# A two-layer diffusion backbone on one core: the squares of the output projections recorded as tasks, and three places moved at the end

## The chip, the cores and the metric

The kernel runs on one core of one Trainium2 chip, as one program. The metric is the device time of one execution in microseconds (us), the median over several executions. Five engines work in parallel, each through its own instructions in order: TensorE (PE, with its weight loads PEld), VectorE (DVE), ScalarE (ACT), GpSimd (POOL), and SyncE (SP), which issues nearly all DMA transfers. An instruction that waits holds up everything behind it on its engine.

## The reference

128 context tokens and 512 latent tokens of width 2048 go through two layers and a last norm. In each layer:

```python
h = rms_norm(x, norm_g[l]) * (1.0 + scale) + shift
y, side = even_mixer(...)  # layer 0: window attention || gated linear attention, times silu(gate)
y, side = odd_mixer(...)   # layer 1: neighbourhood attention || spatial-gating MLP, times silu(gate)
x = x + gate * (y @ w_out[l])
...
y_prompt = rms_norm(x, final_norm_g)

def rms_norm(x, g, eps=1e-6):
    xf = x.astype(jnp.float32)
    y = xf * lax.rsqrt(jnp.mean(xf * xf, axis=-1, keepdims=True) + eps)
    return (y * g.astype(jnp.float32)).astype(x.dtype)
```

The change touches the line `x = x + gate * (y @ w_out[l])`, called the output projection here, the sum of the squares of its result, which the next norm needs, and the last norm. Everything is in float32. The outputs are the two normed results and the keys, values and states of the context.

## The kernel before

**Layout.** Features lie on the 128 partitions, tokens on the free axis: an activation is KT = 16 tiles of 128 x 640 (128 context and 512 latent tokens). A float32 product is made from three passes of a faster format: every operand is split into a high part (`acth`, `whi`, made by ACT) and a low part (`actl`, `wlo`, made by POOL or DVE as the difference), and PE computes hi*hi, hi*lo and lo*hi.

**Weights.** SP loads weights into `wraw` or `rs`; ACT writes `whi`, POOL or DVE writes `wlo`. Both lie in a ring of 2560 columns, so a split can run ahead of PE only as far as PE has freed room. For most pairs of output chunks the kernel uses a Strassen-like scheme (`spair`) with sums of weights, which DVE makes (`wraw<-rs`, `rs<-wraw,rs`, 128 x 768), and sums of activations (`eh`, `el`).

**Folding and reloading.** For this scheme six tiles of the second half of the activations are overwritten ("folded"); their old values (`acth` and `actl`) are kept in DRAM (`bh_dram`, `bl_dram`). `unfold` reloads the six pairs when a stage ends, and sets a flag `uf0` to `uf5` for each; the matmuls that need them come behind the flag.

**Order.** The program is recorded by hand into fixed orders, engine by engine. A planner (`Pace`) keeps an estimated clock for each engine; `tick` is called between matmuls, and lets generator tasks (`spawn`) record their next steps. A task may wait for a flag (`wait`), for data by the planner's clock (`until`), or for an engine to be not too far ahead (`calm`). `need(flag)` lets tasks run, in the recording, until the flag is set. All of this sets only the order of instructions; on the chip they wait for semaphores.

**Output projection.** `out_proj` records 16 output tiles f, as n = 0 to 15. `out_evac` makes two functions for each: `pre` loads the tile of x, and `evac` takes the finished halves from PSUM (`pa`: first 320 tokens, `pb`: the rest), lets DVE write y = gate * p + x into `Y[n % 8]`, stores y, and has `square` record ACT's square and POOL's addition to `ssq` at once. In the profile a square is `arena<-Y` on ACT (128x320), the addition `arena<-arena` on POOL.

**The end.** The last pair of outputs of layer 1 runs through `hpair`, which splits the tokens into a part of 384 and one of 256 and finishes the first part before the second. After each part the task `final(half)` is spawned: it sums the squares over partitions with a matmul against `ones`, computes rstd with Ln and Exp on ACT (their function table is loaded by `tables` if another is active), scales the 16 tiles on DVE and POOL, and writes `o_y`. `reload` fetches tiles that had gone to DRAM. `final(1)` begins behind the flag `prescaled`, which `final(0)` sets at its tile 13 of 0 to 15.

Of the kernel before, what the change touches and what calls it, by code (L numbers as in the profile page):

```python
# [13 lines left out]
AF = mybir.ActivationFunctionType  # L14
ALU = mybir.AluOpType
# [4 lines left out]
KT = D // 128  # L20
# [15 lines left out]
NY = 8  # L36
# [203 lines left out]
class Trunk:  # L240
# [889 lines left out]
    def unfold(self):  # L1130

        nc = self.nc
        for i, j in enumerate(JT):
            for x, y in zip((self.ah, self.al), self.keep):
                self.dma(x[:, j, CW:].bitcast(U32), y[:, j, :].bitcast(U32))
                yield
            self.flags.add(f"uf{i}")
        self.flags.add("unfold")
        self.folded = False
        yield  # L1140
# [828 lines left out]
    def out_evac(self, l, n, f, xsrc, spill):  # L1969
        nc = self.nc  # L1970
        box = {}

        def square(y, c):
            if l == 1 and f == KT - 1:
                nc.scalar.activation(self.sq[:, : c.stop - c.start], y[:, c], AF.Square)
            else:
                self.ssq_add(self.ssq, y, f, self.sq if self.cut == CUT else self.sqs.next(), c)

        def squares(y):
            if n == KT - 1:  # L1980
                yield from self.wait("squares")
            for q, s in ((slice(0, HT), self.sqs.next()), (slice(HT, T), self.sqs.next())):
                yield from self.wait("x1:14")
                yield from self.calm(2.0, "a")
                nc.scalar.activation(s, y[:, q], AF.Square)
                yield from self.until(s)
                yield from self.calm(4.0, "v")
                nc.vector.tensor_tensor(self.ssq[:, q], self.ssq[:, q], s, ALU.add)
                yield
            self.flags.add("squares")  # L1990

        def evac(pa, pb):
            G, at = self.G[l], self.cut
            y = self.Y[:, n % NY, :]
            if pa is not None:
                if n < NY:
                    self.clear(f"Y{n}", "C", "R")
                x = box["x"]
                nc.vector.scalar_tensor_tensor(
                    y[:, 0:NCTX], pa[:, 0:NCTX], G[:, f, 0:1], x[:, 0:NCTX], ALU.mult, ALU.add  # L2000
                )
                nc.vector.scalar_tensor_tensor(
                    y[:, NCTX:at], pa[:, NCTX:at], G[:, f, 1:2], x[:, NCTX:at], ALU.mult, ALU.add
                )
                if pb is None:
                    square(y, slice(0, at))
            if pb is not None:
                x = box["x"]
                nc.vector.scalar_tensor_tensor(
                    y[:, at:T], pb[:, 0 : T - at], G[:, f, 1:2], x[:, at:T], ALU.mult, ALU.add  # L2010
                )
                if l == 0 or n < NY:
                    self.dma(spill[:, f, :], y)
                if l == 0 and n >= KT - 2:
                    return squares(y)
                if pa is not None:
                    square(y, slice(0, at))
                square(y, slice(at, T))

        def pre():  # L2020
            x = box["x"] = self.xr.next()
            self.dma(x, xsrc[:, f, :])

        return pre, evac
# [144 lines left out]
    def program(self):  # L2169
        nc, tc, d, Y = self.nc, self.tc, self.d, self.Y  # L2170
# [25 lines left out]
        def do(f):  # L2196
            acts.append(("f", f))
# [144 lines left out]
        for kv in range(2):  # L2342
# [26 lines left out]
            for h in range(4 * kv, 4 * kv + 4):  # L2369
                if kv and h != 5:  # L2370
                    i = max(h - 5, 0)
# [37 lines left out]
        def out_proj(l, xsrc, sp):  # L2409
            for i, f in enumerate(range(KT) if l else OUT0):  # L2410
                pre, ev = self.out_evac(l, i, f, xsrc, sp)
                add(wout[l, f], 128, False, pre, ev)
                if i == 1:
                    pair("k", STEPS, f"y{l}", f"uo{l}")
                elif i == KT - 3:
                    pairs((KT - 4) // 2)
# [139 lines left out]
        for i in range(2):  # L2556
            y = lambda i=i: L[f"gy{i}"]
# [3 lines left out]
        for n, i in enumerate(GATES):  # L2561
            y = Y[:, n % NY, :]
# [20 lines left out]
        acts.append(k)  # L2583
        do(lambda: self.need("ada_g1"))
        out_proj(1, spill, ysp)
        do(lambda: self.spawn(self.reload()))
        r = acts.pop()
        pair("h", self.final)
        h = acts.pop()
# [56 lines left out]
    def final(self, half):  # L2646
        nc, d, L = self.nc, self.d, self.L
        c = slice(CUT, T) if half else slice(0, CUT)
        n = c.stop - c.start
        t, u = (m[:, :n] for m in L["ms"])  # L2650
        if half:
            yield from self.wait("prescaled")
        p = self.sm()[:, :n]
        r = self.rstd[:, c]
        yield from self.until(self.ssq[:, c])
        self.mm(p, self.ones, self.ssq[:, c], stop=False)
        yield from self.until(self.sq[:, :n])
        self.mm(p, self.ones, self.sq[:, :n], start=False)
        if not half:
            yield 0.8  # L2660
        self.rms(r, p, t)
        q = self.sm()[:, :n]
        nc.vector.scalar_tensor_tensor(q, t, 1.5, r, ALU.add, ALU.mult)
        if half:
            nc.scalar.activation(u, t, AF.Copy, bias=1.5)
            nc.gpsimd.tensor_tensor(u, u, r, ALU.mult)
            self.flush()
        else:
            nc.scalar.activation(u, q, AF.Copy)
            self.flags.add("fr")  # L2670
            yield from self.wait("reload")
        at = 0
        for k in range(KT):
            y, g = self.x2(k)[:, 0, c], self.fg[:, k : k + 1]
            if k in self.POOLED:
                if not half:
                    yield from self.calm(1.5, "a")
                    nc.scalar.activation(self.x2(k), self.x2(k), AF.Copy, scale=g)
                nc.gpsimd.tensor_tensor(y, y, u, ALU.mult)
            else:  # L2680
                nc.vector.scalar_tensor_tensor(y, y, g, q, ALU.mult, ALU.mult)
            if half and (k % 2 or k == 0):
                eng = (nc.sync, self.tc.nc.scalar)[(k + 1) // 2 % 2]
                eng.dma_start(d["o_y"][:, at : k + 1, c], self.x2(at, k + 1 - at)[:, :, c])
                at = k + 1
            elif k % 2 and not half:
                self.dma(d["o_y"][:, k - 1 : k + 1, c], self.x2(k - 1, 2)[:, :, c])
            if not half:
                if k == self.POOLED[-1]:
                    self.flags.add("prescaled")  # L2690
                yield 0.3
        self.flags.add(f"final{half}")
        yield
# [164 lines left out]
```

## Time and profile before

| | |
|---|---|
| median of 3 executions | 2102.5 us (2102.18 to 2102.93) |
| the profiled execution | 2104.64 us, of it span 2102.8 us |
| TensorE clock granted | 0.996 on average |
| busy: PE, DVE, ACT, POOL | 2052.0, 1305.9, 1078.3, 1301.4 us |
| DMA | 340.18 MB, mean 162 GB/s |
| chain that ended last, by engine | PE 79%, DMA 7%, DVE 6%, POOL 3%, issue 3%, ACT 2% |

In a row of the timeline stand the start and the duration in us, the engine, the line, the operation, out<-in with shapes, the count of merged instructions, and in brackets the idle time of the engine before it and who ended it. L214 and L397 are lines of helpers that record every operation, so rows are told apart by their tiles. The first output projection runs from about 880 to 1060 us, the second from about 1890 us to the end.

### The profile page before, as it was taken

To read this page: it belongs to the slowest core of one execution; us is meant where nothing else is said; L and a number is where in the kernel's file an instruction comes from. 1 tells how busy PE (TensorE), PEld (TensorE's weight loads), DVE (VectorE), ACT (ScalarE), POOL (GpSimd) and SP (SyncE) were. 2 spreads that over 40 slices of the span, in tenths; PEclk is the share of its full clock that TensorE was granted. 3 is DMA by queue.
4 is the path that set the end of the run, shared out by engine and by line. 5 is a ranking of instruction groups with operands and counts; after the bars stand their busy time and mean duration, and the time that the engine had idled before them with its cause. 6 is when DMAs were issued, how large, how long until landed. Compare 5 with 4: busy or idle time off the path is not lost.

```text
span 2102.8 us, 40256 instructions
## 1 busy us (share of the span) xinstructions
PE 2052.0 (98%) x14345; PEld 2000.7 (95%) x14345; DVE 1305.9 (62%) x3034; ACT 1078.3 (51%) x2485; POOL 1301.4 (62%) x1090
## 2 busy tenths in 40 slices
PE   7999999999999999999999999999999999999997
PEld 6899999999999999999999999999999999999996
DVE  4746586676465664787376878787454444466434
ACT  5645565554566866543564434444444544454443
POOL 4656565355455563888755656555655577767884
PEclk9999999999999999999999999999999999999998
DMA  9966343335465544565634454444222344363426
GB/s 362 389 218 207 120 140 123 116 116 175 149 200 173 171 162 149 175 211 181 227 126 129 131 167 152 137 149 148 97 75 94 105 134 131 120 224 116 139 93 240
DMA packets 192841, 340.18 MB, mean 162 GB/s; under 512 B 20896, under 2 KB 70144, under 8 KB 192640
## 3 DMA queue, kind: packets, MB, share of 16 engines
q1 hardware_dynamic: 191296, 336.45, 48.4%
q8 instruction: 112, 1.84, 0.4%
q10 hardware_dynamic: 1344, 1.17, 0.2%
q14 instruction: 89, 0.73, 0.1%
HBM read 303.03 MB, written 31.88 MB: 159 GB/s over the span
## 4 chain that ended last, share of the span: by engine, by line
PE 79%; DMA 7%; DVE 6%; POOL 3%; issue 3%; ACT 2%; SPq 1%; ACTq 0%; POOLq 0%; DVEq 0%
PE bank L397 76%; POOL wlo L214 2%; PE bank L402 2%; DVE arena L214 1%; DVE adas L214 1%; DVE Y L214 1%; DMA adas<-gateT 1%; DMA more<-ada 1%; DVE bank L214 1%; ACT arena L214 1%; DMA Y<-xT 1%; DMA adas<-ada 1%; SPq L431 1%; PE bank L1426 1%; POOL actl L214 0%
## 5 line engine op out<-in xcount | busy, mean ns | idle before, releaser
L397 PE MATMUL bank<-acth,whi 128*128 128x320 f32 (+3 forms) x3320 | 1020.9, 318 | 7.3 <-ACT bc L214 3.0
L397 PE MATMUL bank<-acth,wlo 128*128 128x320 f32 (+3 forms) x3320 | 993.9, 310 | 3.2 <-POOL wlo L214 3.0
L397 PE MATMUL bank<-actl,whi 128*128 128x320 f32 (+3 forms) x3320 | 993.2, 310 | 1.1 <-DMA actl<-bl_dram 1.1
L214 POOL TENSOR_TENSOR wlo<-wraw,whi 128x512 fp32r<-128x512 f32 (+1 forms) x446 | 564.5, 1278 | 388.9 <-ACT whi L214 302.3
L397 PEld LDWEIGHTS bank<-acth,whi 128*128 128x128 f32 (+1 forms) x3320 | 617.1, 189 | 16.2 <-ACT bc L214 4.4
L397 PEld LDWEIGHTS bank<-acth,wlo 128*128 128x128 f32 (+1 forms) x3320 | 617.2, 189 | 4.7 <-POOL wlo L214 4.7
L397 PEld LDWEIGHTS bank<-actl,whi 128*128 128x128 f32 (+1 forms) x3320 | 617.2, 189 | 3.2 <-DMA actl<-bl_dram 1.6
L214 POOL TENSOR_TENSOR wlo<-rs,whi 128x384 fp32r<-128x384 f32 x370 | 409.2, 1125 | 190.8 <-ACT whi L214 154.3
L214 ACT ACTIVATE whi<-wraw 128x512 fp32r<-128x512 f32 (+1 forms) x456 | 260.7, 587 | 93.0 <-PE bank L397 66.4
L214 ACT ACTIVATE whi<-rs 128x384 fp32r<-128x384 f32 x370 | 183.3, 517 | 59.4 <-PE bank L397 51.2
L397 PE MATMUL bank<-eh,wlo 128*128 128x322 f32 (+1 forms) x666 | 206.8, 311 | 2.2 <-POOL wlo L214 2.2
L397 PE MATMUL bank<-eh,whi 128*128 128x322 f32 (+1 forms) x666 | 209.0, 314 | 0.0
L397 PE MATMUL bank<-el,whi 128*128 128x322 f32 (+1 forms) x666 | 206.8, 310 | 0.0
L214 DVE TENSOR_TENSOR wraw<-rs 128x768 f32<-128x768 f32 x74 | 99.1, 1339 | 131.6 <-DMA rs<-w_odd 46.6
L214 POOL TENSOR_TENSOR prod<-adas,mixrow 128x512 f32<-128x512 f32 x94 | 123.6, 1324 | 84.4 <-ACT prod L214 59.1
L214 DVE CUSTOM_DVE_ANT_0 adas<-adas,bank,partg 128x256 bf16<-128x256 f32 (+1 forms) x290 | 156.2, 539 | 12.0 <-DMA adas<-ada_g 4.6
L214 ACT ACTIVATE arena<-arena,bc 128x512 f32<-128x512 f32 (+4 forms) x189 | 97.8, 538 | 76.4 <-DVE arena L214 71.3
L397 PEld LDWEIGHTS bank<-eh,wlo 128*128 128x128 f32 x666 | 125.5, 188 | 3.5 <-POOL wlo L214 3.5
L397 PEld LDWEIGHTS bank<-el,whi 128*128 128x128 f32 x666 | 125.8, 189 | 0.0
L397 PEld LDWEIGHTS bank<-eh,whi 128*128 128x128 f32 x666 | 125.5, 188 | 0.1
L214 DVE TENSOR_TENSOR bank<-bank,sums 128x320 f32<-128x320 f32 (+1 forms) x148 | 70.7, 493 | 72.8 <-PE bank L397 56.3
L214 DVE CUSTOM_DVE_ANT_0 adas<-adas,bank,part 128x512 bf16<-128x512 f32 x142 | 105.6, 744 | 9.5 <-DMA adas<-ada 6.9
(221 smaller groups left out, 2467.7 us busy)
## 6 DMA issues: line engine op xcount, KB each, us to landing
wraw<-w_even SPq DMA_DIRECT2D x176, 256.0 KB, 3.4
adas<-ada_g SPq DMA_DIRECT2D x128, 256.0 KB, 3.6
adas<-ada SPq DMA_DIRECT2D x128, 256.0 KB, 3.6
rs<-w_odd SPq DMA_DIRECT2D x50, 384.0 KB, 3.2
wraw<-w_odd SPq DMA_DIRECT2D x74, 256.0 KB, 3.6
wraw<-w_out SPq DMA_DIRECT2D x60, 256.0 KB, 3.5
rs<-w_odd SPq DMA_DIRECT2D x50, 256.0 KB, 3.9
Y<-ada SPq DMA_DIRECT2D x24, 512.0 KB, 7.7
```

The source lines that it names most:

```text
L214: return f(*args, **kw)
L397: self.nc.tensor.matmul(out, lhsT, rhs, start=start, stop=stop, **kw)
L402: self.nc.tensor.transpose(out, in_, self.ident[:k, :k])
L431: self.nc.sync.dma_start(out, in_)
L1426: nc.tensor.matmul(o, c, w, start=j < 4, stop=j >= 12)
```

## The change

There are four edits. (1) For the first 12 of 16 outputs, each half's square becomes a task (`late`) of its own: it waits for the square before it, for y, and for ACT and then POOL to be not far ahead by the planner's clock. `evac` records, ahead of overwriting a slot of Y, that its squares are done, and ahead of the last four outputs that all tasks are. (2) `unfold` yields after a pair, not after each of its two transfers. (3) The Ln/Exp table is loaded where `reload` is spawned. (4) `final(1)` begins behind `final0`, the end of `final(0)`, instead of `prescaled`.

```diff
@@ unfold
             for x, y in zip((self.ah, self.al), self.keep):
                 self.dma(x[:, j, CW:].bitcast(U32), y[:, j, :].bitcast(U32))
-                yield
             self.flags.add(f"uf{i}")
+            yield
@@ out_evac
         def square(y, c):
-            if l == 1 and f == KT - 1:
+            if n < KT - 4:
+                self.spawn(late(y, c, 2 * n + (c.start > 0)))
+            elif l == 1 and f == KT - 1:
                 nc.scalar.activation(self.sq[:, : c.stop - c.start], y[:, c], AF.Square)
             else:
                 self.ssq_add(self.ssq, y, f, self.sq if self.cut == CUT else self.sqs.next(), c)
+
+        def late(y, c, i):
+            yield from self.wait("ssq" if i == 0 else f"sq{l}:{i - 1}")
+            yield from self.until(y[:, c])
+            yield from self.calm(1.0, "a")
+            if i < 2:
+                nc.scalar.activation(self.ssq[:, c], y[:, c], AF.Square)
+            else:
+                s = self.sqs.next()
+                nc.scalar.activation(s, y[:, c], AF.Square)
+                yield from self.until(s)
+                yield from self.calm(1.5, "g")
+                nc.gpsimd.tensor_tensor(self.ssq[:, c], self.ssq[:, c], s, ALU.add)
+            self.flags.add(f"sq{l}:{i}")
+            yield
@@ out_evac, evac
+            if n >= KT - 4:
+                self.need(f"sq{l}:{2 * KT - 9}")
             y = self.Y[:, n % NY, :]
             if pa is not None:
                 if n < NY:
                     self.clear(f"Y{n}", "C", "R")
+                    self.flags.add("ssq")
+                else:
+                    self.need(f"sq{l}:{min(2 * (n - NY) + 1, 2 * KT - 9)}")
@@ program
         out_proj(1, spill, ysp)
-        do(lambda: self.spawn(self.reload()))
+        do(lambda: [self.tables(), self.spawn(self.reload())])
@@ final
         if half:
-            yield from self.wait("prescaled")
+            yield from self.wait("final0")
```

Three places of the new order. PE's order is the same in both. First, ACT at the start of the second output projection (`arena_8164<-Y` are squares, `whi` weight splits, `acth<-bank` high parts of folded activations, `sums` a copy of a product). Before:

```order
L214 ACTIVATE arena_8164<-Y 128x320 x2
L214 ACTIVATE acth<-bank_69 128x320
L214 ACTIVATE whi<-rs_8159 128x384
L214 ACTIVATE sums_8160<-bank_67 128x320
L214 ACTIVATE whi<-wraw 128x384 x2
L214 ACTIVATE whi<-rs_8159 128x384 x2
L214 ACTIVATE arena_8164<-Y 128x320
L214 ACTIVATE whi<-rs_8159 128x384 x2
```

And in the change:

```order
L214 ACTIVATE acth<-bank_69 128x320
L214 ACTIVATE whi<-rs_8159 128x384
L214 ACTIVATE sums_8160<-bank_67 128x320
L214 ACTIVATE whi<-wraw 128x384 x2
L214 ACTIVATE whi<-rs_8159 128x384
L214 ACTIVATE acth<-bank_69 128x320
L214 ACTIVATE whi<-rs_8159 128x384 x3
L214 ACTIVATE whi<-wraw 128x512
L214 ACTIVATE whi<-wraw 128x384
L214 ACTIVATE arena_8164<-Y 128x320
```

The squares of the first outputs have left the splits of the first Strassen pair; the first one now stands behind them.

Second, SP at the last reload of pairs (`acth<-bh_dram` and `actl<-bl_dram` are one pair, `wraw<-w_out` a load of weights, `arena<-x1T_dram` one of x). From the third pair on, before:

```order
L431 DMA actl<-bl_dram 128x320
L431 DMA wraw<-w_out 128x512
L431 DMA acth<-bh_dram 128x320
L431 DMA arena_8164<-x1T_dram 128x640
L431 DMA actl<-bl_dram 128x320
L431 DMA wraw<-w_out 128x512
L431 DMA acth<-bh_dram 128x320
L431 DMA wraw<-w_out 128x512
L431 DMA actl<-bl_dram 128x320
L431 DMA acth<-bh_dram 128x320
L431 DMA wraw<-w_out 128x512
L431 DMA actl<-bl_dram 128x320
```

And in the change:

```order
L431 DMA actl<-bl_dram 128x320
L431 DMA arena_8164<-x1T_dram 128x640
L431 DMA acth<-bh_dram 128x320
L431 DMA actl<-bl_dram 128x320
L431 DMA acth<-bh_dram 128x320
L431 DMA actl<-bl_dram 128x320
L431 DMA acth<-bh_dram 128x320
L431 DMA actl<-bl_dram 128x320
L431 DMA arena_8164<-x1T_dram 128x640
L431 DMA wraw<-w_out 128x512 x3
```

The pairs stand together, and the weight loads come behind them.

Third, the end, on ACT (a piece of the difference: the table load, the splits of the last weights, the squares of the first part, 128x384, its rstd and its scaling):

```order
+L526 ACT_TABLE_LOAD
 L214 ACTIVATE whi<-wraw 128x512 x6
 L214 ACTIVATE arena_8164<-Y 128x384 x2
 L214 ACTIVATE whi<-wraw 128x512
-L526 ACT_TABLE_LOAD
 L214 ACTIVATE rstd<-bank_74,eps 128x384
 L214 ACTIVATE rstd<-rstd 128x384
 L214 ACTIVATE arena_8164<-bank_72 128x384
+L214 ACTIVATE whi<-wraw 128x512
 L214 ACTIVATE rs_8159<-rs_8159,small 128x640
```

The table load has moved ahead of seven splits, and one split ahead of the first scaling. On DVE (`Y<-Y,small,bank_72` are rows of the first part, those of 256 the second part), before:

```order
L214 SCALAR_TENSOR_TENSOR Y<-bank_68,G_99,arena_8164 128x256
L214 SCALAR_TENSOR_TENSOR Y<-Y,small,bank_72 128x384 x2
L214 SCALAR_TENSOR_TENSOR arena_8164<-rstd 128x256
L214 SCALAR_TENSOR_TENSOR arena_8164<-bank_73,arena_8164 128x256
L214 SCALAR_TENSOR_TENSOR bank_74<-arena_8164,rstd 128x256
L214 SCALAR_TENSOR_TENSOR rs_8159<-rs_8159,small,bank_74 128x256 x3
L214 SCALAR_TENSOR_TENSOR arena_8164<-arena_8164,small,bank_74 128x256 x2
L214 SCALAR_TENSOR_TENSOR adas<-adas,small,bank_74 128x256
L214 SCALAR_TENSOR_TENSOR Y<-Y,small,bank_74 128x256 x5
L214 SCALAR_TENSOR_TENSOR Y<-Y,small,bank_72 128x384
```

And in the change:

```order
L214 SCALAR_TENSOR_TENSOR Y<-bank_68,G_99,arena_8164 128x256
L214 SCALAR_TENSOR_TENSOR Y<-Y,small,bank_72 128x384 x3
L214 SCALAR_TENSOR_TENSOR arena_8164<-rstd 128x256
L214 SCALAR_TENSOR_TENSOR arena_8164<-bank_73,arena_8164 128x256
L214 SCALAR_TENSOR_TENSOR bank_74<-arena_8164,rstd 128x256
```

The last row of the first part has moved ahead of the second norm, and its write with it.

## The prediction

> **What bounds the kernel now.** I read the page first, for the shares, then the busy time by stretches of 50 us, then the timeline of TensorE (PE) for every matmul that waited, then the timelines of ScalarE (ACT), GpSimd (POOL), VectorE (DVE) and the sync queue (SP) around those matmuls.
>
> ```profile
> span 2102.8 us, 40256 instructions
> PE 2052.0 (98%) x14345; PEld 2000.7 (95%) x14345; DVE 1305.9 (62%) x3034; ACT 1078.3 (51%) x2485; POOL 1301.4 (62%) x1090
> ```
>
> PE is busy for 98% of the span, so only its gaps, and what comes before its first and after its last matmul, can be won. By stretches (columns: length, PE, PEld, DVE, ACT, POOL busy, clock, DMA share, GB/s):
>
> ```profile
> 950.00:1000.00 50.00, 48.36 (x328) 47.84 (x327) 37.78 (x81) 18.59 (x42) 42.03 (x39) 1.00 0.54 177
> 1900.00:1950.00 50.00, 48.85 (x329) 48.09 (x328) 26.98 (x44) 22.28 (x51) 42.94 (x39) 1.00 0.40 133
> 1950.00:2000.00 50.00, 50.00 (x343) 50.00 (x342) 20.14 (x30) 20.90 (x46) 43.84 (x40) 1.00 0.38 129
> ```
>
> The first two rows lie in the two output projections, which the change touches, and PE has gaps there at full clock; in the third row, the same work later on, it has none, with POOL as busy. So the gaps are matters of order, not of throughput. Every matmul behind a wait, from the first output projection to the last multiplication of weights (in brackets: idle time, and what ended it):
>
> ```profile
> 889.47 0.41 PE L397 MATMUL bank<-eh,wlo 128*128 128x320 f32 x1 [1.02 <-POOL wlo L214]
> 911.58 0.41 PE L397 MATMUL bank<-eh,wlo 128*128 128x320 f32 x1 [0.28 <-POOL wlo L214]
> 917.93 0.41 PE L397 MATMUL bank<-acth,wlo 128*128 128x320 f32 x1 [0.78 <-POOL wlo L214]
> 965.40 0.42 PE L397 MATMUL bank<-eh,wlo 128*128 128x320 f32 x1 [0.86 <-POOL wlo L214]
> 971.76 0.41 PE L397 MATMUL bank<-acth,wlo 128*128 128x320 f32 x1 [0.78 <-POOL wlo L214]
> 1916.74 0.43 PE L397 MATMUL bank<-acth,wlo 128*128 128x320 f32 x1 [1.06 <-POOL wlo L214]
> 2068.09 0.44 PE L397 MATMUL bank<-actl,whi 128*128 128x384 f32 x1 [0.42 <-DMA actl<-bl_dram]
> 2069.61 0.45 PE L397 MATMUL bank<-actl,whi 128*128 128x384 f32 x1 [0.64 <-DMA actl<-bl_dram]
> 2084.93 0.38 PE L397 MATMUL bank<-acth,wlo 128*128 128x256 f32 x1 [0.41 <-POOL wlo L214]
> ```
>
> Six wait for a weight's low part (wlo) in the projections, two for a reloaded low part of an activation (actl), one for a wlo in the last part. A wait costs more than its idle time, since the matmul behind it starts slowly. The matmuls before and after the 2068.09 one:
>
> ```profile
> 2067.16 0.33 PE L397 MATMUL bank<-acth,wlo 128*128 128x384 f32 x1
> 2067.34 0.33 PE L397 MATMUL bank<-acth,whi 128*128 128x384 f32 x1
> 2068.36 0.33 PE L397 MATMUL bank<-acth,wlo 128*128 128x384 f32 x1
> ```
>
> Starts are 0.18 us apart without a wait. Here the two steps around the wait take 0.75 and 0.27, together 0.66 over the usual 0.36, for an idle time of 0.42: each wait costs its idle time and 0.24.
>
> **Edit 1: the squares as tasks.** Now ACT squares a half of an output at once, and POOL adds it to ssq. ACT and POOL serve their instructions in order, and the weight splits stand behind the square. Around the waits at 917.93 and 1916.74:
>
> ```profile
> 915.50 0.47 ACT L214 ACTIVATE arena<-Y 128x320 f32<-128x320 f32 x1 [5.36 <-DVE Y L214]
> 915.88 0.93 ACT L214 ACTIVATE whi<-rs 128x384 fp32r<-128x384 f32 x2
> 916.05 0.87 POOL L214 TENSOR_TENSOR arena<-arena 128x320 f32<-128x320 f32 x1 [0.89 <-PE bank L397]
> 916.88 1.97 POOL L214 TENSOR_TENSOR wlo<-rs,whi 128x384 fp32r<-128x384 f32 x2
> 1914.17 0.47 ACT L214 ACTIVATE arena<-Y 128x320 f32<-128x320 f32 x1 [4.51 <-DVE Y L214]
> 1914.72 1.02 POOL L214 TENSOR_TENSOR arena<-arena 128x320 f32<-128x320 f32 x1 [0.89 <-ACT arena L214]
> 1915.70 1.96 POOL L214 TENSOR_TENSOR wlo<-rs,whi 128x384 fp32r<-128x384 f32 x2
> ```
>
> The square (arena<-Y) waits for DVE's evacuation, the split (whi<-rs) sits behind it, then POOL does the 0.87 us add, then the first wlo, which ends at 916.88 + 1.97/2 = 917.87, and PE starts at 917.93. The new order has no square at these places: the split goes ahead, by the 0.87 of the add at least, more than the 0.78 that PE waited. At 1916.74 it is 1.02 for 1.06, and ACT's own 0.47 besides. The waits at 889.47 and 971.76 are of the same kind. These four go: 1.02 + 0.78 + 0.78 + 1.06 = 3.64, with 4 x 0.24 makes 4.6 us. The other two, 911.58 and 965.40, stand at a pair's end, where DVE now makes the add of the next weights behind the evacuations instead of ahead of them; I count them at nothing and keep their 0.28 + 0.86 + 2 x 0.24 = 1.6 for the range. No instruction is added: 24 squares a layer stay 24, only their places change. The new waits order the recording and are no instructions; what stands behind a moved POOL add is a wlo of a later weight. Between the projections nothing moves but the reloads of pairs, and PE's order is the same throughout, so the time won is kept if the other engines follow.
>
> **Edits 2 and 3: pairs and table.** The reloads, the first part's norm and the end:
>
> ```profile
> 2064.21 0.63 ACT L214 ACTIVATE whi<-wraw 128x512 fp32r<-128x512 f32 x1 [3.54 <-PE bank L397]
> 2065.40 0.32 SPq L431 DMA_DIRECT2D actl<-bl_dram  x1
> 2076.34 0.81 PE L397 MATMUL bank<-arena,ones 128*128 128x384 f32 x2
> 2076.42 0.63 ACT L214 ACTIVATE whi<-wraw 128x512 fp32r<-128x512 f32 x1 [0.59 <-PE bank L397]
> 2077.07 1.28 ACT L526 ACT_TABLE_LOAD   x1
> 2078.36 0.58 ACT L214 ACTIVATE rstd<-bank,eps 128x384 f32<-128x384 f32 x1
> 2087.83 0.48 DVE L214 SCALAR_TENSOR_TENSOR Y<-bank,G,arena 128x256 f32<-128x256 f32 x1 [0.44 <-PE bank L397]
> 2090.81 0.50 DVE L214 SCALAR_TENSOR_TENSOR arena<-rstd 128x256 f32<-128x256 f32 x1 [1.45 <-ACT rstd L214]
> 2094.63 2.56 DVE L214 SCALAR_TENSOR_TENSOR Y<-Y,small,bank 128x256 f32<-128x256 f32 x6
> 2097.47 1.09 SPq L431 DMA_DIRECT2D o_y<-Y  x1
> ```
>
> The last actl is issued at 2065.40 and PE starts on it at 2069.61, 4.2 later. In the new order all six pairs stand ahead of four of the weight loads that now lie between them. At 0.32 an issue the last actl comes at least 1.3 us sooner, more where a load waits for its slot; 0.64 + 0.24 would do. Both waits go: 0.42 + 0.64 + 2 x 0.24 = 1.54. The loads that are passed come later by the pairs put ahead of them, some 0.3 each; the split at 2064.21 waited 3.54 for PE's room and not for its load, so that is covered. At the other two reloads of pairs PE does not wait, so nothing there.
>
> The table load lies between the last matmul of the first part's sum, 2076.34 + 0.81 = 2077.15, and rstd at 2078.36. Loaded earlier, rstd starts at 2077.15 - 1.54 = 2075.6, a gain of 2.75 for the first part. In its new place, some 20 us earlier, its 1.28 lies ahead of the splits:
>
> ```profile
> 2055.77 0.34 PE L397 MATMUL bank<-acth,whi 128*128 128x384 f32 x1
> 2058.76 1.28 DVE L214 TENSOR_TENSOR wlo<-wraw,whi 128x512 fp32r<-128x512 f32 x1 [1.12 <-ACT whi L214]
> ```
>
> The next split ends at 2060.04, and PE comes to it after three units of 12 matmuls at 0.175, at about 2061.9: 1.9 of slack against 1.28. So it costs nothing, or 0.3 if the slack is misjudged. The Trainium skill (ScalarE: Activation LUTs, "What ACT_TABLE_LOAD costs") puts a switch at 1.28 and a drain of 1.38, 2.66 in all. The trace has the 1.28 and no drain: rstd starts 0.01 after the load.
>
> The split behind the wait at 2084.93 goes ahead of the scaling on ACT and POOL, and the first part ends sooner, so that wait goes as well: 0.41 + 0.24 = 0.65. So PE ends 1.54 + 0.65 = 2.2 sooner, and DVE, which waits for it at 2087.83, passes the 2.2 on to the second part's norm.
>
> **Edit 4: the last part waits for all of the first.** Now the first part's last row is the sixth of DVE's six and its write, of 384 KB, is issued last, at 2097.47. The queues then are full (the GB/s of 40 slices of 2090 to 2103):
>
> ```profile
> GB/s 312 378 326 392 373 336 378 378 378 340 38 258 281 268 50 321 366 312 369 328 347 344 334 359 312 353 347 340 340 334 347 377 373 369 236 0 0 0 0 0
> ```
>
> At about 345 GB/s these 393,216 bytes take 1.1 us of the end. In the new order the row is made before the second norm, in the 1.45 that DVE waits there, and the write goes into the free slices. Gain 1.1, between 0.4 (DVE's sixth op alone, 2.56/6) and 1.5. The wait that this adds holds back only the recording of the second norm: behind it on DVE are that norm's operations, one row later than now, on ACT nothing new.
>
> **Sum.** 4.6 + 2.2 + 1.1 = 7.9 us. The profiled execution took 2104.64 (span 2102.8 and 1.8 around it), 2.1 over the median of 2102.5; the gain applies to both: 2096.7 in a profile, 2102.5 - 7.9 = 2094.6 for the median.
>
> **Rivals.** A difference of 0.2%, 4.2 us, is about what a measurement here can tell from none. (a) The adds stall other splits: the order puts them singly among splits, with a wide DVE add beside some.
>
> ```profile
> 922.25 0.89 POOL L214 TENSOR_TENSOR arena<-arena 128x320 f32<-128x320 f32 x1 [0.20 <-ACT arena L214]
> 956.72 0.96 DVE L214 TENSOR_TENSOR wraw<-rs 128x768 f32<-128x768 f32 x1
> 966.35 1.75 DVE L214 TENSOR_TENSOR wraw<-rs 128x768 f32<-128x768 f32 x1 [0.40 <-POOL wlo L214]
> ```
>
> An add takes 0.89, a wide add 0.96 or, beside POOL's work, 1.75. If four new waits of 0.9 + 0.24 come up, the 4.6 is given back and the end's 3.3 is left: 2099.2. For it: POOL is busy 42 of 50 us. Against: PE has no gap from 1950 to 2000 with the same adds. The Trainium skill (SBUF — State Buffer, on the shared port pair) says that a two-input DVE operation and a POOL operation exclude each other for the whole instruction; the 0.96 and 1.75 agree, and it speaks for this rival. (b) The end is bound by writing: half-1 rows and 345 GB/s set it, and only about 0.8 of the 3.3 comes through: 2102.5 - 5.4 = 2097.1. For it are the full slices above, against it that they begin only once rows are ready. (c) Slower: the late adds wedge in front of the very wlo that PE wants. 22 a layer are late adds, 44 in all; with 0.89 + 0.24 = 1.13 each, the 7.9 and 4.2 more are eaten from 11 such waits on; with 14 it is 2102.5 + 15.8 - 7.9 = 2110.4. Against it: the whole projection has six now. (d) The change does not do it: SP waits for PE before all pairs alike, and the squares' new places still wait for DVE: 2102.5. The new order has pairs and squares apart, so this is unlikely. (e) The table load holds ACT for longer than its own 1.28 in its new place, say for twice that: 2.56 against 1.9 of slack, 0.7 lost, 2095.3; the 0.01 above speaks against it. The skill's 2.66 would be this case, with 0.8 lost.
>
> **Numbers.** Forecast 0.56, (a) 0.14, (b) 0.17, (c) 0.06, (d) 0.03, (e) 0.04. Faster are the forecast, (b) and (e): 0.77; the same (a) and (d): 0.17; slower (c): 0.06. The range goes from 2102.5 - 7.9 - 1.6 - 0.95 = 2092.05 (the two waits left out; 2.75 instead of 2.2 from the first part; 1.5 instead of 1.1 for the write), taken as 2091.8, up to 2099.5, which takes in (a); outside are (c), (d) and some edges.
>
> **What would show it.** In the new profile: no PE wait for wlo at 889, 917, 971 and 1916 (less what was won); no PE wait for actl near 2068; the table load ahead of the last six splits and rstd right behind the sum's matmul; the last write of 256 KB. Wrong would be waits for wlo at new places worth over 4 us, or an end no shorter than now from DVE's last evacuation, 2102.8 - 2087.8 = 15.0.

## The result, and the profile after

The changed kernel took 2096.15 us (median of 6 runs, 2090.79 to 2097.64), the kernel before 2102.34 beside it (2100.2 to 2107.03): a ratio of 0.9968, 95% interval 0.9957 to 0.9979. That is 6.2 us faster, where 7.9 were forecast, and inside the range. The interval goes from 4.4 to 9.0 us and holds both numbers, so the medians alone don't tell 6.2 from 7.9; the difference is read from marks in the profiles below. The profiled execution has a span of 2095.9 us against 2102.8.

```profile
span 2095.9 us, 40282 instructions
PE 2053.0 (98%) x14345; PEld 2004.3 (96%) x14345; DVE 1310.3 (63%) x3034; ACT 1081.6 (52%) x2485; POOL 1294.4 (62%) x1090
```

The numbers of PE's, DVE's, ACT's and POOL's instructions are as before, and their busy times within 7 us: nothing was saved, work was moved. Single runs of one kernel differ by up to 7 us, so a change of 1 us has to be read inside the profile. Three marks serve for this in every run: the matmul at the head of the first output projection (848.95 before), DVE's last add of bank and sums in the second (2055.97), and the end of the span. The timelines of DVE and PE in the changed kernel have them at

```profile
848.26 0.72 PE L397 MATMUL bank<-acth,whi 128*128 128x320 f32 x2 [0.59 <-ACT eh L214]
2052.29 0.50 DVE L214 TENSOR_TENSOR bank<-bank,sums 128x320 f32<-128x320 f32 x1 [1.69 <-PE bank L397]
```

The **long stretch** between the first two marks, which holds both projections, went from 1207.0 to 1204.0 (3.0 won); the **tail** from the second mark to the end of the span from 46.8 to 43.6 (3.2 won). The other 0.7 of the 6.9 lies ahead of the first mark. It is taken as the drift of one execution, since that mark stands anywhere from 845.7 to 850.7 in the profiles of all runs. The 6.2 that are left agree with the medians, to the tenth by chance.

Every matmul of the changed kernel that waited 0.25 or more in the places that the prediction listed, from PE's timeline:

```profile
889.77 0.41 PE L397 MATMUL bank<-acth,whi 128*128 128x320 f32 x1 [0.29 <-ACT whi L214]
890.85 0.41 PE L397 MATMUL bank<-acth,wlo 128*128 128x320 f32 x1 [0.52 <-POOL wlo L214]
1911.39 0.42 PE L397 MATMUL bank<-eh,wlo 128*128 128x320 f32 x1 [0.45 <-POOL wlo L214]
```

Nine waits have become three. But these three are not remainders of the old ones: the first two came up a few matmuls behind the one that had waited at 889.47, the third some 30 matmuls ahead of the one that had waited at 1916.74. By stretches of 50 us PE's gaps have shrunk without closing (48.36 and 48.85 busy before):

```profile
950.00:1000.00 50.00, 49.76 (x336) 49.17 (x336) 37.27 (x76) 20.79 (x45) 44.25 (x41) 1.00 0.58 189
1900.00:1950.00 50.00, 49.34 (x331) 48.41 (x330) 28.74 (x40) 23.03 (x53) 43.74 (x40) 1.00 0.41 128
```

The tail, from the timelines of ACT, DVE and SP:

```profile
2054.54 1.28 ACT L526 ACT_TABLE_LOAD   x1
2055.84 2.19 ACT L214 ACTIVATE whi<-wraw 128x512 fp32r<-128x512 f32 x4
2071.05 0.63 ACT L214 ACTIVATE whi<-wraw 128x512 fp32r<-128x512 f32 x1 [0.59 <-PE bank L397]
2071.82 0.58 ACT L214 ACTIVATE rstd<-bank,eps 128x384 f32<-128x384 f32 x1
2081.80 0.48 DVE L214 SCALAR_TENSOR_TENSOR Y<-bank,G,arena 128x256 f32<-128x256 f32 x1 [0.63 <-PE bank L397]
2088.42 2.04 DVE L214 SCALAR_TENSOR_TENSOR Y<-Y,small,bank 128x256 f32<-128x256 f32 x5
2089.76 1.67 SPq L2706 DMA_DIRECT2D o_y<-Y  x2
```

The load lies ahead of the last splits, the first part's rstd follows the sum's matmul without it, DVE's last evacuation stands at 2081.80 (29.5 behind the second mark; before 2087.83, 31.9), DVE makes five rows at the end instead of six, and the last writes are of 256 KB.

### The profile page after: what moved, and what is told of

It reads as the page before. It is cut to its first block, busy times and chain, and to the rows that moved or that the text cites. A ratio compares the mean times of both kernels' runs of the same rounds, so it can differ in the third digit from the quotient of the medians.

```text
span 2095.9 us, 40282 instructions
## 1 busy us (share of the span) xinstructions
PE 2053.0 (98%) x14345; PEld 2004.3 (96%) x14345; DVE 1310.3 (63%) x3034; ACT 1081.6 (52%) x2485; POOL 1294.4 (62%) x1090
## 4 chain that ended last, share of the span: by engine, by line
PE 87%; DMA 4%; DVE 3%; POOL 2%; ACT 2%; issue 2%; SPq 0%; ACTq 0%; POOLq 0%; DVEq 0%
PE bank L397 84%; PE bank L402 2%; POOL wlo L214 1%; DVE arena L214 1%; DMA more<-ada 1%; DMA Y<-xT 1%; DVE adas L214 1%; ACT arena L214 1%; DMA adas<-shift_s 1%; PE bank L1426 1%; DVE Y L214 0%; POOL actl L214 0%; DMA raw<-crow_s 0%; DMA adas<-crow 0%; DMA adas<-gateT 0%
```

## The experiments

Each edit was run alone on the kernel before, two of them together, and then single suspects on the changed kernel. All times of the table are us; the rstd columns count from the second mark to the start of the first and of the second part's rstd on ACT.

| run | ratio to before (95%) | long stretch | first rstd | second rstd | tail |
|---|---|---|---|---|---|
| before | 1 | 1207.0 | 22.39 | 33.89 | 46.83 |
| changed | 0.9968 (0.9957 to 0.9979) | 1204.0 | 19.53 | 31.35 | 43.61 |
| squares alone | 0.9991 (0.9981 to 1.0000) | 1204.5 | 22.50 | 33.99 | 46.96 |
| pairs alone | 1.0000 (0.9991 to 1.0010) | 1207.4 | 20.70 | 32.20 | 45.88 |
| table alone | 1.0011 (1.0002 to 1.0021) | 1207.1 | 25.82 | 37.65 | 50.55 |
| write alone | 0.9994 (0.9984 to 1.0004) | 1207.3 | 22.47 | 33.96 | 46.15 |
| pairs and table | 0.9994 (0.9985 to 1.0003) | 1206.3 | 19.52 | 31.35 | 44.62 |
| changed, late squares left out | 0.9963 (0.9949 to 0.9976) | 1203.0 | 19.52 | 31.36 | 43.57 |
| changed, fewer writes | 0.9973 (0.9964 to 0.9983) | 1204.7 | 19.53 | 31.36 | 43.12 |
| changed, scaling early | 0.9969 (0.9956 to 0.9982) | 1203.4 | 19.52 | 31.29 | 43.45 |
| changed, products held | 0.9970 (0.9960 to 0.9981) | 1204.2 | 19.52 | 31.34 | 43.62 |
| changed, both of these | 0.9973 (0.9962 to 0.9983) | 1204.3 | 19.52 | 31.30 | 43.55 |
| changed, again | 0.9971 (0.9961 to 0.9981) | 1204.2 | 19.52 | 31.35 | 43.56 |
| changed, two table loads | one run | 1204.3 | 19.53 | 31.35 | 43.58 |

The five runs without edit 1 have long stretches of 1206.3 to 1207.4, mean 1207.0, and the eight with all its squares 1203.4 to 1204.7, mean 1204.2: the two groups do not overlap, and single profiles scatter by some 0.4.

**Squares alone.** The kernel before with edit 1: `spawn(late(...))` for n below KT - 4, the task `late`, and its two `need` lines.

> The kernel before with edit 1 alone. Two stretches are read from the profile: the long one, from the PE wait at the head of the first output projection (848.95 before, 848.26 after) to DVE's last add of bank and sums in the second (2055.97 and 2052.29), 1207.0 us before and 1204.0 after; and the tail, from there to the span's end, 46.8 before and 43.6 after. Theory 1, the edits add up: the long stretch is 1204.0 +-0.3, the tail 46.8 +-0.3, the time 3.0 lower (ratio 0.9986). The waits left over in the changed kernel (889.77, 890.85, 1911.39) stand at the same places. Theory 2, edit 1 also shifts the planner's order of the last reloads: the tail moves by over 0.5. Theory 3, part of the gain in the long stretch comes from the other edits' ordering of the early reloads: the long stretch stays at 1205 or above.

The long stretch is 1204.5, the tail 46.96, and the three waits stand at the same matmuls with the same idle times (0.28, 0.52, 0.45). Theory 1 holds, with a long stretch 0.2 beyond its margin, which is less than the scatter: edit 1 is worth 2.5 in this profile and 2.8 in the means of the two groups (3.0 from before to changed), all of it in the projections, and no part of the other edits shows in it.

**Pairs alone.**

```
-                self.dma(x[:, j, CW:]..., y[:, j, :]...)
-                yield
             self.flags.add(f"uf{i}")
+            yield
```

> The kernel before with edit 2 alone, the pairs reloaded together. Theory 1: both PE waits for actl near 2068 and 2069.6 go, 1.54 us, the wait for wlo near 2084.9 stays (it hangs on the scaling, which only the table moves), long stretch 1207.0, tail 45.3 +-0.3. Theory 2: the wlo wait goes as well, tail 44.6. Theory 3, the pairs hold back the weights that SP now issues later: a PE wait for a weight of the last part comes up and the tail stays over 46.3.

The two actl waits are gone, the wlo wait stays (0.41, at 2084.19), and the second rstd comes 1.69 sooner, a little more than the 1.54 of theory 1. The tail gave back 0.74 of it and lost only 0.95, outside theory 1's 45.3 +-0.3: the last 384 KB are issued 1.69 sooner too, but the span ends 6.07 behind their issue instead of 5.33. Why that is longer is left open. The time did not show a gain (ratio 1.0000, 95% 0.9991 to 1.0010).

**Table alone.**

```
-        do(lambda: self.spawn(self.reload()))
+        do(lambda: [self.tables(), self.spawn(self.reload())])
```

> The kernel before with edit 3 alone, the table loaded at the reload. Theory 1: the first part's rstd starts right behind the sum's matmul, 1.28 sooner, but the end hangs on PE's last matmul, which this does not move: tail 46.8 to 46.1 (46.1 if the wlo wait near 2084.9, 0.41 + 0.24, goes). Theory 2: in the order on SP the last pairs now stand behind one weight load more than before, so that the actl waits near 2068 grow by 0.3 or more each: tail 47.1 or more, slower than before. Theory 3, the load costs ACT more than its 1.28 in its new place: a PE wait for a split between 2058 and 2066.

Theory 2, and far beyond its 47.1: the tail grew by 3.7. PE's timeline at the place of the two old actl waits:

```profile
2068.52 0.44 PE L397 MATMUL bank<-acth,whi 128*128 128x384 f32 x1 [1.35 <-DMA acth<-bh_dram]
2070.06 0.45 PE L397 MATMUL bank<-acth,whi 128*128 128x384 f32 x1 [0.46 <-DMA acth<-bh_dram]
2071.16 0.69 PE L397 MATMUL bank<-actl,whi 128*128 128x384 f32 x1 [0.65 <-DMA actl<-bl_dram]
```

The planner charges the load to ACT's clock, and with that SP's order changes: one weight load more stands ahead of the last pairs, and the next to last acth is issued 7.47 behind the second mark where it was 6.42, so that acth itself is late. The last pair in SP's timeline, each half behind a weight load:

```profile
2064.07 0.38 SPq L431 DMA_DIRECT2D wraw<-w_out  x1
2064.55 0.38 SPq L431 DMA_DIRECT2D acth<-bh_dram  x1
2065.44 0.33 SPq L431 DMA_DIRECT2D wraw<-w_out  x1
2065.82 0.42 SPq L431 DMA_DIRECT2D actl<-bl_dram  x1
```

The waits are 2.46 against 1.06, each with its restart (the 0.24 of the prediction). The rest is mostly PE's clock. By stretches of 2 us (granted clock third from the end):

```profile
2068.20:2070.20 2.00, 1.20 (x4) 0.62 (x4) 0.00 (x0) 0.00 (x0) 0.00 (x0) 1.00 1.06 402
2070.20:2072.20 2.00, 1.35 (x4) 1.09 (x5) 0.00 (x0) 0.00 (x0) 0.00 (x0) 0.54 1.02 420
2072.20:2074.20 2.00, 2.00 (x7) 2.00 (x7) 0.74 (x2) 0.52 (x1) 0.56 (x1) 0.50 1.01 412
2074.20:2076.20 2.00, 2.00 (x8) 2.00 (x8) 0.00 (x0) 0.00 (x0) 0.43 (x1) 0.50 0.78 310
2076.20:2078.20 2.00, 2.00 (x11) 2.00 (x10) 0.00 (x0) 0.00 (x0) 0.00 (x0) 0.75 0.05 20
```

For some 6 us behind the waits matmuls start 0.32 apart instead of 0.175, as two of them in PE's timeline; 17 make 2.5 us.

```profile
2072.92 0.52 PE L397 MATMUL bank<-acth,whi 128*128 128x384 f32 x1
2073.24 0.52 PE L397 MATMUL bank<-actl,whi 128*128 128x384 f32 x1
```

Waits 1.4 longer, one restart more (0.24) and these 2.5 make 4.1; the wlo wait of the last part is gone here, which gives 0.65 back, and 3.5 of the 3.76 at the second rstd are accounted for. So waits here can cost far more than their idle time and 0.24 each, and edit 3 by itself is a loss (ratio 1.0011). Whether the executions without a profile lost the clock as well is not shown.

**Write alone.**

```
-            yield from self.wait("prescaled")
+            yield from self.wait("final0")
```

> The kernel before with edit 4 alone, the second part's norm behind the first part's last row. Theory 1: the last 384 KB are written ahead of the second part's and the tail is shorter by 0.7 to 1.1, 45.7 to 46.1; all else as before. Theory 2, the end is bound by the bytes that the queues still have to write after the second norm's rows begin, whatever their order: tail 46.8 +-0.3. Theory 3, DVE's one row more ahead of the second norm holds that norm back by 0.4: tail 47.2.

The second rstd is unmoved (33.96) and the tail 46.15, 0.68 shorter, just under theory 1's 0.7; theories 2 and 3 fall. Between 37 and 39 us behind the second mark the queues of the kernel before moved only 115 to 289 GB/s by stretches of 0.5 us; here they moved 329 to 378 GB/s there.

**Pairs and table.**

> The kernel before with edits 2 and 3 together. Alone, edit 2 shortened the way from the last add of bank and sums to the second part's rstd by 1.69 (33.89 to 32.20) and edit 3 lengthened it by 3.76, since SP then issues the last pairs behind the weight loads. Theory 1, edit 3's loss is SP's order and the joined pairs take it away: no PE wait for acth or actl near 2068, rstd of the first part 19.5 behind that add, of the second 31.35, as in the changed kernel; tail 44.3 +-0.3 (the changed kernel's 43.6 and edit 4's 0.7). Theory 2, the table load costs something in its place all the same: PE waits for a split there, second rstd at 32.2 or later. Theory 3, the end is bound by the bytes to be written: rstd comes sooner as in theory 1 but the tail stays at 45.5 or more.

Theory 1: no wait near 2068, rstd at 19.52 and 31.35, tail 44.62, at the very edge of its 44.3 +-0.3. In SP's timeline no weight load stands any more between the last four pairs, and the table's loss of 3.76 at the second rstd becomes a gain of 0.85 (32.20 to 31.35). The wlo wait of 0.41 is gone, which with its restart is 0.65 of this. From here to the changed kernel the tail falls by 1.0, so edit 4 is worth 0.7 alone and 1.0 beside the others.

**Late squares left out.** In the changed kernel the late squares of outputs 1 to 11 are not made; the rest stands.

```
-                self.spawn(late(y, c, 2 * n + (c.start > 0)))
+                if n == 0:
+                    self.spawn(late(y, c, int(c.start > 0)))
+                else:
+                    self.flags.add(f"sq{l}:{2 * n + (c.start > 0)}")
```

> The changed kernel without the late squares of outputs 1 to 11 of each layer, ScalarE's squares and GpSimd's adds both (so the sum behind the norm is not the reference's). Theory 1, the waits left over in the projections (889.77, 890.85, 1911.39, and small ones) come from the place of splits behind other work and not from the moved adds: they stay, long stretch 1204.0 +-0.3. Theory 2, the moved adds stall the splits (the first rival): they go, and the long stretch falls to 1202.0 or below, which is the 1.7 that the forecast's 4.6 for the squares was too large by.

The waits that were to tell are all there, in PE's timeline:

```profile
888.78 0.41 PE L397 MATMUL bank<-acth,whi 128*128 128x320 f32 x1 [0.28 <-ACT whi L214]
889.87 0.41 PE L397 MATMUL bank<-acth,wlo 128*128 128x320 f32 x1 [0.52 <-POOL wlo L214]
1909.52 0.41 PE L397 MATMUL bank<-eh,wlo 128*128 128x320 f32 x1 [0.47 <-POOL wlo L214]
```

So they do not come from the moved adds. The long stretch is 1203.0, between the theories: 1.2 under the mean of the eight, with only one profile for it. Beside the three, the changed kernel has matmuls at 967.91 and 970.98 that start 0.26 and 0.30 late, and these are gone here; some 1.2 us is the most that the late squares and adds still cost together, the first rival's mechanism at a quarter of its price.

**Fewer writes.** The changed kernel writes the first part's rows only for k below NY.

> The changed kernel without the four writes of the first part's rows 8 to 15 (1.57 MB, left out of the output). Theory 1, the end is bound by the queues, which are full from 2083.9 on at about 345 GB/s: with 4.5 us less to write the tail falls from 43.6 until the second part's rows set it, by 2 to 3 us. Theory 2, the second part's rows set it already: the last write is issued at the same place and the tail stays within 0.4 of 43.6.

Theory 2 nearly: 1.57 MB less, 4.5 us of writing at 345 GB/s, shorten the tail by 0.5. The GB/s of 40 slices of the last 16.8 us, with fewer writes:

```profile
GB/s 0 307 384 340 340 399 362 373 304 0 20 0 0 0 0 0 0 0 0 0 5 298 307 81 327 344 349 337 349 341 346 327 351 341 349 341 203 0 0 0
```

The queues stand empty for 4 us ahead of the second part and still end within 0.5 us of where they did. Its own 2.1 MB at about 340 GB/s, which begin with its first row, fill the slices up to the end, so they are what sets it by these rows; no run wrote fewer of them. What the first part leaves in the queues is worth 0.5.

**Scaling early.** ACT's scaling of rows 9, 11 and 13 in a loop at the end of `reload` instead of in `final`.

> The changed kernel with ScalarE's scaling of rows 9, 11 and 13 moved from behind the first norm to the reload, where ScalarE waits (5.19 us near 2058, 3.67 near 2066). If the end is bound by the queues: GpSimd's three products of those rows come 1.5 to 2.5 sooner, the gap in the writing from 2082.2 to 2083.9 fills, and the tail falls from 43.6 by 1.0 to 1.7. If the second part's rows set the end: no change within 0.4. If ScalarE's scaling in the new place delays a square or a split: the first rstd comes later by up to 0.8 and the gain is gone.

43.45: no change, as the run before this one implies, and second rstd at 31.29.

**Products held.** One line ahead of the first projection puts the due time of the low-priority task, VectorE's modulation products, 45 us back: `self.low[0] = max(self.low[0], self.now) + 45.0`.

> The changed kernel with the low-priority modulation products on VectorE (adas and part, 0.74 + 0.08 each) held back until some 20 us into the first output projection. In the changed kernel VectorE is busy for 9.76 of the 10 us from 880 to 890 and 9.79 of the next 10, and ScalarE waits 4.87 for it with the weight splits behind. Theory 1, the waits left at 885.5, 889.77 and 890.85 (0.36 + 0.55 + 0.79 with restarts) are VectorE's jam and not the squares': they go, and the long stretch falls from about 1204.2 to 1202.5. Theory 2, the jam is not the cause, or it only moves to where the products come now: the long stretch stays within 0.5 of 1204.2.

Theory 2. The products left the place, and two waits of much the same length came up all the same, 1.9 us sooner behind the first mark, which stands at 846.52 here (PE's and ACT's timelines):

```profile
886.10 0.41 PE L397 MATMUL bank<-eh,whi 128*128 128x320 f32 x1 [0.21 <-ACT whi L214]
887.18 0.41 PE L397 MATMUL bank<-eh,wlo 128*128 128x320 f32 x1 [0.52 <-POOL wlo L214]
```

```profile
885.20 0.44 ACT L214 ACTIVATE acth<-bank 128x320 fp32r<-128x320 f32 x1 [2.55 <-DVE bank L214]
885.54 1.34 ACT L214 ACTIVATE whi<-rs 128x384 fp32r<-128x384 f32 x3
```

In the changed kernel ACT's timeline reads the same at 888.87:

```profile
888.87 0.44 ACT L214 ACTIVATE acth<-bank 128x320 fp32r<-128x320 f32 x1 [4.87 <-DVE bank L214]
889.20 0.93 ACT L214 ACTIVATE whi<-rs 128x384 fp32r<-128x384 f32 x2
```

In both, the split (whi) stands on ACT behind the rounding of a folded activation (acth<-bank), which waits for a chain of three adds on DVE. In the kernel before, the same rounding (the fifth of the projection, by count) stood behind these splits:

```profile
886.95 0.47 ACT L214 ACTIVATE arena<-Y 128x320 f32<-128x320 f32 x1 [1.92 <-DVE Y L214]
887.33 1.34 ACT L214 ACTIVATE whi<-rs 128x384 fp32r<-128x384 f32 x3
891.86 0.44 ACT L214 ACTIVATE acth<-bank 128x320 fp32r<-128x320 f32 x1 [2.26 <-DVE bank L214]
```

The wait at 1911.39 has the same picture. In the changed kernel the rounding stands ahead of the splits and waits for DVE:

```profile
1909.40 0.44 ACT L214 ACTIVATE acth<-bank 128x320 fp32r<-128x320 f32 x1 [4.35 <-DVE bank L214]
1909.73 1.34 ACT L214 ACTIVATE whi<-rs 128x384 fp32r<-128x384 f32 x3
```

In the kernel before it came at 1916.11, behind them. So all three waits that are left lie behind a rounding that the new order has put ahead of a split. That this order makes the wait is what the rows say; no run moved the rounding back, so it is not shown.

**Both variants, and the changed kernel again.**

> The kernel with the products held back and the scaling of rows 9, 11 and 13 moved to the reload as well. If both work as they did or are expected to alone: long stretch 1202.5, tail 43.45, about 1.8 under the changed kernel. If the head of the projection keeps its waits: long stretch 1204.2 and no measurable difference from the changed kernel.

> The changed kernel once more, beside the two variants on the same chip: long stretch 1204.2 +-0.5, tail 43.6 +-0.2, ratio to before 0.9968 +-0.001.

The combination keeps its waits at 886.62 and 887.70 and does not beat the changed kernel (0.9973 beside 0.9971). The changed kernel repeated to 0.15 us in both stretches of the profile.

**Two table loads.**

```
-        do(lambda: [self.tables(), ...
+        do(lambda: [tc.nc.scalar.preload_act_table_set("exp_and_others"), self.tables(), ...
```

> The changed kernel with one more table load of 1.28 (another set) ahead of the moved one, and nothing else moved on any engine. Theory 1, the forecast's slack of 1.9 at that place: the two loads take 2.56, TensorE waits about 0.7 for a split between 2056 and 2062 and restarts, the second rstd comes 0.9 later (32.2 behind the last add of bank and sums instead of 31.35). Theory 2, the slack is larger: no wait, 31.35. Theory 3, the slack is used up by the one load already: 1.3 to 1.5 later.

Theory 2: no wait, second rstd at 31.35. ACT's timeline:

```profile
2053.78 1.28 ACT L2608 ACT_TABLE_LOAD   x1
2055.06 1.28 ACT L526 ACT_TABLE_LOAD   x1
2056.36 1.15 ACT L214 ACTIVATE whi<-wraw 128x512 fp32r<-128x512 f32 x2
```

The place covers 2.56, where the forecast gave it 1.9.

## Why the prediction was right, point by point

**Squares: 4.6 forecast, 2.8 to 3.0 measured.** The mechanism (a split behind a square and an add) was right: the waits at 917.93 and 971.76 went and nothing came in their place, and at 889.47 and 1916.74 too the split that PE waited for moved ahead. The step that failed is the one from "these four go" to a gain of their full price: it did not look up what the new order puts ahead of the next split. There a rounding that waits for DVE, which had followed the splits, came to stand ahead of one. At the first place 1.02 of idle became 0.29 + 0.52 with one restart more, and nothing was won; at the second 1.06 became 0.45. The listing of ACT's new order ahead of the prediction has this rounding: its second acth<-bank stands ahead of three splits, and the order before shows none there. By their prices the four gave 2.6 instead of 4.6. Against that, 911.58 and 965.40, counted at nothing, went all but small rests and gave 1.6. Matmuls that start 0.24 to 0.30 late became more, five (885.52, 967.91, 970.98, 1905.34 and 1913.09) instead of two, and took 0.8. That makes 3.4, within the scatter of the 3.0. That the miss is not larger is in part luck: the two waits that were counted at nothing gave back most of the 2.0 that the four fell short by. The first rival's mechanism, adds that stall splits, was at most 1.2 us of the shortfall (late squares left out).

**Pairs: 1.54 forecast, 1.69 measured**, both waits gone.

**Table: 1.21 sooner for the first part (2.75 less the pairs' 1.54) and 0.65 through the wlo wait for the second; measured 1.18 (20.70 to 19.52) and 0.85 (32.20 to 31.35).** Together with the pairs the first part's rstd gained 2.86, where 2.75 stood, and the second's 2.54, where 2.2 stood. "So it costs nothing" was right with more slack than the working had: three units of 12 matmuls at 0.175 from 2055.77 end at 2062.07 and not at 2061.9, which makes its slack 2.0, and two loads of 2.56 still fitted. The prediction added the edits up as if they were independent, and that step would have failed for edit 3 by itself: it loses 3.76 at the second rstd unless the pairs are joined. Only the order of the whole change, which the prediction read, keeps that from showing.

**Write: 1.1 forecast, 0.7 to 1.0 measured.** The mechanism held: the write goes into slices in which the queues had room (write alone).

**The rival of the end bound by writing** was right in its mechanism, that the second part's rows and some 340 GB/s set the end, and wrong in its price. It let 0.8 of the 3.3 come through, and 3.2 did, since what brings the first of these rows sooner is passed on: the second rstd came 2.54 sooner by pairs and table, and 2.54 + 0.68 (write alone) is the 3.2 of the tail. Without edit 4 only 2.2 of the 2.54 came through; why is not shown.

**The extra price of a load in its new place**, the rival of 2.56 against 1.9, fell twice: a second load is a second 1.28, and both fit. The Trainium skill (ScalarE: Activation LUTs, "What ACT_TABLE_LOAD costs") has 1.38 of drain beside the 1.28 of a load. The rows do not agree: the two loads start 1.28 apart, and the next ACT instruction starts 0.02 behind the second.

The sum: 7.9 forecast; 3.0 + 3.2 = 6.2 measured. The tail's 3.3 came out at 3.2, and the miss lies in the squares. In the tail too two sizes were off in opposite ways, 2.54 at the second rstd for 2.2 and 0.7 for the write's 1.1, so that the agreement to 0.1 is luck.

## What to carry to other kernels

When an instruction goes from ahead of a late one in a queue, look up in the new order what then stands next ahead of it, and ahead of the ones that follow, and whether that waits for the same engine: a wait counts as gained only when the next rows are clear too. Test a bundle of edits for its parts before keeping some of them, because in a kernel whose order comes from a planner one edit can be a loss without its neighbour. Where single runs scatter by more than an edit is worth, marks inside the profile that are bound by one busy engine give its price to a few tenths of a microsecond.

## What the hardware showed that was not expected

Behind three short PE waits (1.35, 0.46 and 0.65 within 4 us) the granted clock fell from 1.00 to 0.50 for about 6 us, in the run with the table alone; behind the two of 0.42 and 0.64 in the kernel before it stayed at 1.00, as it did behind 0.51 and 0.66 with the squares alone. The Trainium skill (TensorE: Matmul & The Clock Gate, Part 1) has the clock halve after an idle window of about 3.4 us. Here no single gap was longer than 1.35; that the three together brought the clock down is what this one profile suggests, and no run tested it.

The first add of DVE's three-add chain, which reads acth and actl and not a PSUM bank, takes longer than the others while GpSimd works. The timelines of DVE and of POOL in the run with the products held:

```profile
883.06 1.04 DVE L214 TENSOR_TENSOR bank<-acth,actl 128x320 f32<-128x320 f32 x1
884.13 0.50 DVE L214 TENSOR_TENSOR bank<-bank,acth 128x320 f32<-128x320 f32 x1
```

```profile
882.73 1.01 POOL L214 TENSOR_TENSOR wlo<-rs,whi 128x384 fp32r<-128x384 f32 x1 [1.17 <-ACT whi L214]
```

The add begins under GpSimd's subtraction, which ends at 883.74, and ends 0.36 behind it. In the changed kernel the same kind of add, with GpSimd idle, takes 0.49:

```profile
875.84 0.49 DVE L214 TENSOR_TENSOR bank<-acth,actl 128x320 f32<-128x320 f32 x1
```

The Trainium skill (SBUF — State Buffer, "SBUF: two separate sides") states that a DVE operation with two SBUF inputs and a GpSimd operation that reads SBUF exclude each other for a whole instruction. These rows agree. The prediction weighed it only for the wide adds; here it lengthens the chain for which ScalarE waits, with the split behind it.
